# The last 32 of 384 dense tokens of a PEER layer take their up products from gathered rows; one comparison for both one-hots, a gate copy in runs of four, down products in pairs

## The chip, the cores and the metric

The kernel runs on one core of one Trainium2 chip. The metric is the device time of one execution in microseconds (us), the median over several runs. The engines are PE (TensorE: matmuls, with its weight loads as PEld), DVE (VectorE), ACT (ScalarE), POOL (GpSimd) and SP (SyncE, which issues most DMAs). Numbers are fp32. A product of two fp32 operands is computed here as three matmuls of rounded halves: a tensor is split into a rounded part (`_h`, made by ACT) and the rest (`_l`, made by DVE), and h\*h + h\*l + l\*h is summed in PSUM. Only the gate matmuls below take fp32 operands as they are; in the trace four of them leave eight matmul records, two passes each.

## The reference

The program is an encoder of two layers on 512 tokens of 1024 numbers. Layer 1 mixes tokens by neighbourhood attention, layer 2 by a short convolution; each is followed by a PEER channel mixer, which is what the change touches:

```python
q = (xc @ w_query).reshape(c, 8, 2, 128)
sc = jnp.einsum('chpd,hpnd->chpn', q, sub_keys)      # 128 scores on each of two sides
sv, si = lax.top_k(sc, 16)
cand = sv[:, :, 0, :, None] + sv[:, :, 1, None, :]
cidx = si[:, :, 0, :, None] * 128 + si[:, :, 1, None, :]
best, pos = lax.top_k(cand, 16)
eidx = jnp.take_along_axis(cidx, pos, axis=-1)       # 8 x 16 experts of 16384
g = jax.nn.softmax(best, axis=-1)
a = jnp.einsum('cd,chkd->chk', xc, w_up[eidx])
act = jax.nn.gelu(a, approximate=False) * g
return jnp.einsum('chk,chkd->cd', act, w_down[eidx])
```

Each token uses 128 of the 16384 experts; an expert is a row of w_up and a row of w_down.

## The kernel before

A PEER layer (`peer(l)`) treats its 512 tokens, in four chunks of 128, in two ways. The last chunk (`c3`) gathers: for each of its 128 choices k one indirect DMA of POOL fetches a row of w_up per token (`fetch`, `gather_up`), DVE multiplies it with the normed token `hn` and sums, and later a row of w_down is fetched, scaled and added to `accg` (`gather_down`). The 256 gathers of a layer share four buffers `row`. The other 384 tokens (TD) are dense: all 16384 experts are computed for them in 128 blocks of 128 experts, and a gate matrix that is zero for experts that a token didn't choose weighs the results.

A layer runs in these stages, whose times in the first layer are those of the profiled execution:

- Query (309 to 404 us): up matmuls of the query and key scores `ps_k`, and DVE's first top 16.
- Selections (404 to 512): `retrieval()` runs `select` for chunks 3, 0, 1, 2, which is DVE's work throughout (top 16 of the candidates, the two sides `ii` and `jj` of the choice by masks `msk`). For the dense chunks the gates and both sides are transposed into gT, iT and jT.
- Gate stage (512 to 716): 96 quads of four tokens. For each token a one-hot of side i (`ob`) and one of side j scaled by the gate (`oa`) are made, and one matmul of the two gives the token's 128 x 128 gate matrix, in PSUM bank `ps_gb`. ACT copies the four of a quad into `stage`, and every 32 tokens (GT) the stage goes to DRAM as `gd`.
- Experts (732 to 1552): for each block b `dense_up` computes 24 up matmuls (8 slices of 1024 by three products) over 384 columns, and Gelu leaves `ab`. `dense_down` loads the block's gates (`gt`, four blocks in a load), multiplies (`w`), splits w into w_h and w_l, and adds 18 down matmuls of 512 columns into six PSUM accumulators `acc`. `gt` can't be loaded before the last `gd` is written, and the first down matmul waits for that.

Because DVE and ACT are busy in the selections and gates while PE has little to do there, the first NPRE = 52 ups run in those stages, parked in DRAM as `ad` and read back as `at`. Two numbers a step say how much of them PE takes: each step of `retrieval` yields its estimated DVE time and PE time, and ups are emitted until PE's sum reaches PRE_RATE times DVE's. Later ups run AHEAD = 4 blocks ahead of the downs. The lists `fresh` and `kept` interleave blocks computed late and parked blocks. A scheduler then orders each engine's instructions within its limits by pool buffers and dependencies, so that the order on an engine isn't that of the code:

```python
for d, p in retrieval():
    dve += d
    pe += p
    while pe < dve * PRE_RATE and next(pre, 0) is None:
        pe += 0.49
for _ in pre:
    pass
```

Each engine runs its instructions in order, and SP's queue takes all loads of weights, gates and parked blocks in order too; the gathers are issued by POOL.

## Time and profile before

| What | Value |
|---|---|
| median of 3 runs | 3018.89 us (3018.78 to 3021.11) |
| the profiled execution | 3024.75 us |
| its span | 3023.0 us |
| mean granted TensorE clock | 0.996 |
| PE busy | 2978.8 us, 99% |
| DVE busy | 2343.2 us, 78% |
| ACT busy | 1361.7 us, 45% |
| POOL busy | 657.6 us, 22% |
| DMA | 747.94 MB, mean 247 GB/s |

The profile counts an engine as busy from an instruction's start to its end, and matmuls overlap, so the duration of one is longer than the pitch at which they follow each other. Line numbers are those of the kernel printed above. A share over the whole span is a mean over stages that are bound by different things.

### The profile page before, as it was taken

To read this page: it belongs to the slowest core of one execution; us is meant where nothing else is said; L and a number is where in the kernel's file an instruction comes from. 1 tells how busy PE (TensorE), PEld (TensorE's weight loads), DVE (VectorE), ACT (ScalarE), POOL (GpSimd) and SP (SyncE) were. 2 spreads that over 40 slices of the span, in tenths; PEclk is the share of its full clock that TensorE was granted. 3 is DMA by queue.
4 is the path that set the end of the run, shared out by engine and by line. 5 is a ranking of instruction groups with operands and counts; after the bars stand their busy time and mean duration, and the time that the engine had idled before them with its cause. 6 is when DMAs were issued, how large, how long until landed. Compare 5 with 4: busy or idle time off the path is not lost.

```text
span 3023.0 us, 43875 instructions
## 1 busy us (share of the span) xinstructions
PE 2978.8 (99%) x15602; PEld 2665.3 (88%) x15602; DVE 2343.2 (78%) x5115; ACT 1361.7 (45%) x2237; POOL 657.6 (22%) x571
## 2 busy tenths in 40 slices
PE   8999999999999999999999999999999999999998
PEld 6887899999888888888878879999988888888886
DVE  4445899887888888887874489998688888888786
ACT  4444246996333333333342233599733333333333
POOL 0000000001434443443400000000044344444341
PEclk9999999999999999999999999999999999999999
DMA  4332244667999999998943323556699999999994
GB/s 157 98 98 88 95 137 156 228 222 297 337 344 336 336 343 340 338 335 315 331 144 98 108 93 122 163 203 231 246 354 344 333 351 333 338 329 343 331 327 174
DMA packets 297980, 747.94 MB, mean 247 GB/s; under 512 B 23456, under 2 KB 139168, under 8 KB 294688
## 3 DMA queue, kind: packets, MB, share of 16 engines
q1 hardware_dynamic: 224032, 476.67, 45.4%
q0 software_dynamic: 73728, 268.47, 24.0%
q8 instruction: 123, 2.02, 0.3%
q14 instruction: 97, 0.79, 0.1%
HBM read 672.17 MB, written 72.88 MB: 246 GB/s over the span
## 4 chain that ended last, share of the span: by engine, by line
PE 93%; DVE 4%; DMA 1%; issue 1%; ACT 1%; DVEq 0%; ACTq 0%; SPq 0%
PE ps_up L127 46%; PE acc L536 34%; PE ps_gb L457 6%; PE ps_o L191 3%; PE ps_s L261 1%; DVE wu_l L106 1%; PE ps_o L293 1%; PE ps_k L398 1%; PE ps_t L175 1%; PE ps_pt L280 1%; DMA wd_raw<-in_down 1%; DVE tk L595 0%; ACT sq L150 0%; DMA gd<-stage 0%; PE ps_v L239 0%
## 5 line engine op out<-in xcount | busy, mean ns | idle before, releaser
L127 PE MATMUL ps_up<-xhf,wu_l 128*128 128x384 f32 (+1 forms) x2304 | 798.8, 347 | 1.1 <-DVE wu_l L106 1.0
L127 PE MATMUL ps_up<-xhf,wu_h 128*128 128x384 f32 (+1 forms) x2304 | 794.3, 345 | 2.3 <-ACT ab L499 2.0
L127 PE MATMUL ps_up<-xlf,wu_h 128*128 128x384 f32 (+1 forms) x2304 | 792.6, 344 | 0.0
L105 ACT ACTIVATE wu_h<-wu_raw 128x1024 fp32r<-128x1024 f32 x336 | 355.4, 1058 | 712.2 <-PE ps_up L127 435.1
L536 PE MATMUL acc<-wd_h,w_l 128*128 128x512 f32 x1536 | 604.0, 393 | 0.0
L470 POOL DMA_INDIRECT row<-in_up,eidx x256 | 322.3, 1259 | 1277.5 <-DMA wu_raw<-in_up_t 424.7
L536 PE MATMUL acc<-wd_l,w_h 128*128 128x512 f32 x1536 | 599.2, 390 | 0.0
L105 ACT ACTIVATE wd_h<-wd_raw 128x1024 fp32r<-128x1024 f32 x256 | 271.6, 1061 | 703.6 <-issue 619.4
L106 DVE TENSOR_TENSOR wu_l<-wu_raw,wu_h 128x1024 fp32r<-128x1024 f32 x336 | 409.9, 1220 | 172.5 <-ACT wu_h L105 171.2
L536 PE MATMUL acc<-wd_h,w_h 128*128 128x512 f32 x1536 | 516.5, 393 | 2.9 <-ACT w_h L105 2.9
L106 DVE TENSOR_TENSOR wd_l<-wd_raw,wd_h 128x1024 fp32r<-128x1024 f32 x256 | 313.4, 1224 | 241.8 <-ACT wd_h L105 228.8
L127 PEld LDWEIGHTS ps_up<-xhf,wu_h 128*128 128x128 f32 x2304 | 433.3, 188 | 21.8 <-ACT ab L499 3.3
L127 PEld LDWEIGHTS ps_up<-xlf,wu_h 128*128 128x128 f32 x2304 | 433.1, 188 | 17.5
L127 PEld LDWEIGHTS ps_up<-xhf,wu_l 128*128 128x128 f32 x2304 | 433.1, 188 | 17.3 <-DVE wu_l L106 4.0
L470 POOL DMA_INDIRECT row<-in_down,eidx x256 | 329.4, 1287 | 517.7 <-DVE sq L477 470.7
L536 PEld LDWEIGHTS acc<-wd_l,w_h 128*128 128x128 f32 x1536 | 288.5, 188 | 61.9
L536 PEld LDWEIGHTS acc<-wd_h,w_h 128*128 128x128 f32 x1536 | 287.8, 188 | 58.7 <-ACT w_h L105 3.6
L536 PEld LDWEIGHTS acc<-wd_h,w_l 128*128 128x128 f32 x1536 | 288.9, 188 | 54.8 <-DVE w_l L106 0.4
L486 DVE SCALAR_TENSOR_TENSOR accg<-row,ag,accg 128x1024 f32<-128x1024 f32 x256 | 327.4, 1279 | 11.3 <-DMA row<-in_down,eidx 10.5
L477 DVE SCALAR_TENSOR_TENSOR sq<-row,hn 128x1024 bf16<-128x1024 f32 x256 | 311.9, 1218 | 3.7 <-DMA row<-in_up,eidx 2.3
L457 PE MATMUL ps_gb<-ob,oa 128*128 128x128 f32 x1536 | 209.6, 274 | 0.0
L458 ACT ACTIVATE stage<-ps_gb 128x512 f32<-128x512 f32 x192 | 204.6, 1114 | 2.1 <-PE ps_gb L457 1.3
(164 smaller groups left out, 3307.0 us busy)
## 6 DMA issues: line engine op xcount, KB each, us to landing
wd_raw<-in_down SPq DMA_DIRECT2D x256, 512.0 KB
wu_raw<-in_up_t SPq DMA_DIRECT2D x256, 512.0 KB
gd<-stage SPq DMA_DIRECT2D x24, 2048.0 KB
gt<-gd SPq DMA_DIRECT2D x64, 768.0 KB
ad<-ab SPq DMA_DIRECT2D x104, 192.0 KB
at<-ad SPq DMA_DIRECT2D x52, 384.0 KB
...
```

What stands on the lines that cost most here:

```text
L105: nc.scalar.activation(hi, raw, AF.Copy)
L106: nc.vector.tensor_tensor(lo, raw, hi.bitcast(F32), op=ALU.subtract)
L127: nc.tensor.matmul(ps[:, :n], a[:, c], b[:, kc, :n], start=k == 0, stop=k == 3 * KC - 1)
L175: nc.tensor.transpose(ps[k][:, c * P:(c + 1) * P], hs[c][:, kc * P:(kc + 1) * P], ident)
L191: nc.tensor.matmul(ps[c], a[:, m, c * P:(c + 1) * P], b, start=m == 0 and i == 0, stop=m == KC - 1 and i == 2)
L261: nc.tensor.matmul(ps[:, a * 256:(a + 1) * 256], t["q"][hs, j * P:(j + 1) * P], kk[hs, :, BAND0[j]:BAND0[j] + BAND], start=True, stop=True)
L457: nc.tensor.matmul(ps[:, n * NK:(n + 1) * NK], a, b4[:, n], start=True, stop=True)
L458: nc.scalar.activation(stage[:, :, 4 * q:4 * q + 4].rearrange("p i t -> p t i"), ps.rearrange("p (t i) -> p t i", t=4), AF.Copy)
L470: nc.gpsimd.indirect_dma_start(out=t, out_offset=None, in_=table, in_offset=bass.IndirectOffsetOnAxis(ap=eidx[:, k:k + 1], axis=0))
L477: nc.vector.scalar_tensor_tensor(o, t, 1.0, hn, op0=ALU.mult, op1=ALU.mult, accum_out=ag[:, k:k + 1])
L486: nc.vector.scalar_tensor_tensor(accg, t, ag[:, k:k + 1], accg, op0=ALU.mult, op1=ALU.add)
L536: nc.tensor.matmul(acc[c, half], aa[:, cs], ww[:, hs], start=new and i == 0, stop=n == NK - 1 and ww is held[-1][-1])
```

## The change

Of the 384 dense tokens the last 32 (UT) no longer pass through the dense ups, which shrink to TU = 352 columns. Their up products come from gathered rows: partition 32g + t holds token t and the choices of group g, so that 32 indirect DMAs (`urow`) and 32 DVE products with `hu`, the normed tokens in all four quarters, give all 128 choices of 32 tokens. Gelu and gate are applied to these 128 x 32 values, and the result takes the place of the gate in gT; in the down product their `ab` columns are 1.0. So that the ids are there early, the chunk of these tokens (`cu`) is selected first, then c3. The first 36 gathers of c3 (EARLY) follow the 32 in retrieval, in the three buffers that the loads of down rows use later. One DVE comparison of 1024 elements makes both one-hots of a quad, and ACT scales all four. The gate copy writes runs of four tokens and reads PSUM with a stride of 128. 80 ups are parked (NPRE), at a rate of 1.5; gates are loaded for eight blocks at once (GB), and the product w and its split are made for two blocks at once. The reciprocal root of c3's norm is kept and not computed twice. The core of the diff:

```diff
-NPRE = 52
-PRE_RATE = 1.4
+NPRE = 80
+UN = 1
+UT = 32
+TU = TD - UN * UT
+GB = 8
+PRE_RATE = 1.5
 OB = 12
-ACTN = 2
+EARLY = 36
...
+            cu = ND - 1
+            hu = []
+            for u in range(UN):
+                q = slice(P - (UN - u) * UT, P - (UN - u - 1) * UT)
+                t = wpool.tile([P, D], F32, name="hu", tag="wd_h", bufs=2)
+                nc.sync.dma_start(t[q], g_ffn_row[l].to_broadcast([UT, D]))
+                nc.vector.scalar_tensor_tensor(t[q], h[q, cu], rs[cu][q], t[q], op0=ALU.mult, op1=ALU.mult)
+                for g in range(P // UT):
+                    if g * UT != q.start:
+                        nc.scalar.activation(t[g * UT:(g + 1) * UT], t[q], AF.Copy)
+                hu.append((q, t))
...
+            def unit_lists(gg, ii, jj):
+                flat_ids(eid, ii, jj)
+                for u, (q, _) in enumerate(hu):
+                    for g in range(P // UT):
+                        ks = slice(g * UT, (g + 1) * UT)
+                        nc.scalar.activation(fu[ks, u], eid[q, ks], AF.Copy)
+                        nc.scalar.activation(gu[ks, u], gg[q, ks], AF.Copy)
+                nc.vector.tensor_copy(xu, fu)
+            def unit_steps():
+                at = [(u, k) for u in range(UN) for k in range(UT)]
+                for n in range(len(at) + 2):
+                    if n < len(at):
+                        u, k = at[n]
+                        t = wpool.tile([P, D], F32, name="urow", tag="wd_r", bufs=RAW)
+                        nc.gpsimd.indirect_dma_start(
+                            out=t, out_offset=None, in_=up,
+                            in_offset=bass.IndirectOffsetOnAxis(ap=xu[:, u, k:k + 1], axis=0))
+                        urows.append(t)
+                    if n >= 2:
+                        u, k = at[n - 2]
+                        o = acts.tile([P, D], BF16, name="sq", tag="sq")
+                        nc.vector.scalar_tensor_tensor(o, urows.pop(0), 1.0, hu[u][1], op0=ALU.mult, op1=ALU.mult,
+                                                       accum_out=au[:, u, k:k + 1])
+                    yield
+            def unit_values():
+                nc.scalar.activation(au, au, AF.Gelu)
+                nc.vector.tensor_tensor(au, au, gu, op=ALU.mult)
+                ps = ps_acc("ps_u")
+                for u in range(UN):
+                    nc.tensor.transpose(ps[:UT, u * P:(u + 1) * P], au[:, u], ident)
+                for u in range(UN):
+                    for g in range(P // UT):
+                        ks = slice(g * UT, (g + 1) * UT)
+                        nc.scalar.activation(gT[ks, TU + u * UT:TU + (u + 1) * UT],
+                                             ps[:UT, u * P + g * UT:u * P + (g + 1) * UT], AF.Copy)
...
             def retrieval():
-                for c in (3, 0, 1, 2):
+                units = iter(())
+                for c in (cu, c3, 0, 1):
                     it = select(sv[:, c], si[:, c], pr, cand)
                     while True:
                         try:
                             yield next(it), 0.0
+                            for _ in itertools.islice(units, 1):
+                                yield 1.3, 0.0
...
                     else:
                         ps = ps_acc("ps_g")
                         for n, t in enumerate((gg, ii, jj)):
                             nc.tensor.transpose(ps[:, n * P:(n + 1) * P], t, ident)
-                        for n, t in enumerate((gT, iT, jT)):
-                            nc.vector.tensor_copy(t[:, c * P:(c + 1) * P], ps[:, n * P:(n + 1) * P])
+                        for n, t in enumerate((gT, ijT[:, 0], ijT[:, 1])):
+                            m = min(P, TU - c * P) if n == 0 else P
+                            nc.vector.tensor_copy(t[:, c * P:c * P + m], ps[:, n * P:n * P + m])
+                        if c == cu:
+                            unit_lists(gg, ii, jj)
+                            units = itertools.chain(unit_steps(), early_steps())
...
                 for t0 in range(0, TD, GT):
+                    if t0 == TU:
+                        for _ in units:
+                            yield 1.3, 0.0
+                        unit_values()
                     stage = pr.tile([P, NK, GT], F32, name="stage", tag="big")
                     for q in range(GT // 4):
                         ps = ps_acc("ps_gb")
                         t = t0 + 4 * q
-                        b4 = pr.tile([P, 4, NK], F32, name="ob", bufs=OB // 4)
-                        nc.vector.tensor_tensor(b4, iota[:, None, :].to_broadcast([P, 4, NK]),
-                                                iT[:, t:t + 4, None].to_broadcast([P, 4, NK]), op=ALU.is_equal)
-                        a4 = pr.tile([P, 4, NK], F32, name="oa", bufs=OB // 4)
-                        if ACTN:
-                            nc.vector.tensor_tensor(a4[:, :ACTN], iota[:, None, :].to_broadcast([P, ACTN, NK]),
-                                                    jT[:, t:t + ACTN, None].to_broadcast([P, ACTN, NK]),
-                                                    op=ALU.is_equal)
+                        hot = pr.tile([P, 2, 4, NK], F32, name="hot", bufs=OB // 4)
+                        nc.vector.tensor_tensor(hot, iota[:, None, None, :].to_broadcast([P, 2, 4, NK]),
+                                                ijT[:, :, t:t + 4, None].to_broadcast([P, 2, 4, NK]),
+                                                op=ALU.is_equal)
                         for n in range(4):
-                            a, t = a4[:, n], t0 + 4 * q + n
-                            if n < ACTN:
-                                nc.scalar.activation(a, a, AF.Copy, scale=gT[:, t:t + 1])
-                            else:
-                                nc.vector.tensor_scalar(a, iota, jT[:, t:t + 1], gT[:, t:t + 1],
-                                                        op0=ALU.is_equal, op1=ALU.mult)
-                            nc.tensor.matmul(ps[:, n * NK:(n + 1) * NK], a, b4[:, n], start=True, stop=True)
-                        nc.scalar.activation(stage[:, :, 4 * q:4 * q + 4].rearrange("p i t -> p t i"),
-                                             ps.rearrange("p (t i) -> p t i", t=4), AF.Copy)
-                        yield 1.35, 0.9
+                            a = hot[:, 1, n]
+                            nc.scalar.activation(a, a, AF.Copy, scale=gT[:, t + n:t + n + 1])
+                            nc.tensor.matmul(ps[:, n * NK:(n + 1) * NK], a, hot[:, 0, n], start=True, stop=True)
+                        nc.scalar.activation(stage[:, :, 4 * q:4 * q + 4],
+                                             ps.rearrange("p (t i) -> p i t", t=4), AF.Copy)
+                        yield 1.0, 0.9
+                        for _ in itertools.islice(units, 1):
+                            yield 1.3, 0.0
                     nc.sync.dma_start(gd[t0 // GT], stage)
...
+            ring = [pp.tile([P, 2, TD], F32, name=f"ab{n}") for n in range(AHEAD // 2 + 1)]
+            for t in ring:
+                nc.gpsimd.memset(t[:, :, TU:], 1.0)
...
+            def early_steps():
+                uses = []
+                for n in range(EARLY + 2):
+                    if n < EARLY:
+                        fn, k = gathers[n]
+                        uses.append(fn(k, wpool.tile([P, D], F32, name="erow", tag="wd_r", bufs=RAW)))
+                    if n >= 2:
+                        uses.pop(0)()
+                    yield
             def dense_up(b):
-                for ps in up_pieces(up_t[l, b], xh, xl, TD):
+                for ps in up_pieces(up_t[l, b], xh, xl, TU):
                     yield
-                a = pp.tile([P, TD], F32, name="ab", tag="ab", bufs=AHEAD + 2)
-                nc.scalar.activation(a, ps[:, :TD], AF.Gelu)
-                if b < NPRE:
-                    nc.sync.dma_start(ad[b // 2, :, b % 2], a)
-                else:
-                    ab[b] = a
+                a = ring[b // 2 % len(ring)]
+                nc.scalar.activation(a[:, b % 2, :TU], ps[:, :TU], AF.Gelu)
+                if b % 2:
+                    if b < NPRE:
+                        nc.sync.dma_start(ad[b // 2], a[:, :, :TU])
+                    else:
+                        ab[b - 1] = a
...
             def dense_down(n, b):
-                if b % 4 == 0:
-                    gt = p2.tile([P, TD // GT, 4, GT], F32, name="gt")
+                if b % GB == 0:
+                    gt = p2.tile([P, TD // GT, GB, GT], F32, name="gt")
                     nc.sync.dma_start(gt.rearrange("p g i c -> p g (i c)"),
-                                      gd[:, :, b:b + 4].rearrange("g j i c -> j g (i c)"))
+                                      gd[:, :, b:b + GB].rearrange("g j i c -> j g (i c)"))
                     first.append(gt)
-                if b < NPRE and b % 2 == 0:
-                    at = p2.tile([P, 2, TD], F32, name="at")
-                    nc.sync.dma_start(at, ad[b // 2])
-                    ab[b], ab[b + 1] = at[:, 0], at[:, 1]
-                gt = first[-1]
-                w = p2.tile([P, TD], F32, name="w", bufs=1)
-                mark = nc.vector.tensor_tensor(w.rearrange("p (g c) -> p g c", c=GT),
-                                        ab.pop(b).rearrange("p (g c) -> p g c", c=GT), gt[:, :, b % 4], op=ALU.mult)
-                a_h, a_l = split(w, [P, TD], "w", "w", pool=p2)
+                if b % 2 == 0:
+                    if b < NPRE:
+                        at = parked[b // 2 % 2]
+                        nc.sync.dma_start(at[:, :, :TU], ad[b // 2])
+                        ab[b] = at
+                    w = p2.tile([P, 2, TD], F32, name="w", bufs=1)
+                    mark = nc.vector.tensor_tensor(w.rearrange("p i (g c) -> p i g c", c=GT),
+                                            ab.pop(b).rearrange("p i (g c) -> p i g c", c=GT),
+                                            first[-1][:, :, b % GB:b % GB + 2].rearrange("p g i c -> p i g c"),
+                                            op=ALU.mult)
+                    pair.append((mark, *split(w, [P, 2, TD], "w", "w", pool=p2)))
+                mark, a_h, a_l = pair[-1]
+                a_h, a_l = a_h[:, b % 2], a_l[:, b % 2]
...
```

On DVE in the selections of layer 1, before, between two low halves of up blocks (`wu_l`) stand only steps of `select` (msk, pos, tk, best and ds are its tables):

```order
L106 TENSOR_TENSOR wu_l<-wu_raw,wu_h 128x1024
L638 TENSOR_TENSOR msk<-msk,ds 128x2048
L597 MAX_INDEX pos<-best,tk 128x8 x2
L595 MATCH_REPLACE tk<-best,cand 128x60
L643 TENSOR_TENSOR msk<-msk 128x128x8
L624 COPY ds<-sf 128x16
L595 MATCH_REPLACE tk<-best,cand 128x60
L625 TENSOR_TENSOR ds<-sf 128x16x15
L596 MAX best<-tk 128x8
L644 TENSOR_TENSOR msk<-msk 128x128x4
L106 TENSOR_TENSOR wu_l<-wu_raw,wu_h 128x1024
```

After, in the selection that follows, rows gathered in `urow` and multiplied with `hu` stand there too:

```order
L464 SCALAR_TENSOR_TENSOR sq,au<-urow,hu 128x1024
L113 TENSOR_TENSOR wu_l<-wu_raw,wu_h 128x1024
L695 MAX best<-tk 128x8 x3
L737 TENSOR_TENSOR msk<-msk,ds 128x2048
L464 SCALAR_TENSOR_TENSOR sq,au<-urow,hu 128x1024
L696 MAX_INDEX pos<-best,tk 128x8 x3
L113 TENSOR_TENSOR wu_l<-wu_raw,wu_h 128x1024
L742 TENSOR_TENSOR msk<-msk 128x128x8
L723 COPY ds<-sf 128x16
L724 TENSOR_TENSOR ds<-sf 128x16x15
L464 SCALAR_TENSOR_TENSOR sq,au<-urow,hu 128x1024
L694 MATCH_REPLACE tk<-best,cand 128x60 x2
L113 TENSOR_TENSOR wu_l<-wu_raw,wu_h 128x1024
```

From the last key scores to the first gate matmul a layer has 25 wu_l before, and 36 wu_l and 25 products of L464 after; on PE the ups in that stretch go from 601 to 867. On PE at the end of the gate stage of layer 1, before, 95 ups (ps_up) stand between the last gate matmuls (ps_gb) and the first down matmul (acc):

```order
L457 MATMUL ps_gb<-ob,oa 128x128 x4
L127 MATMUL ps_up<-xhf_2453,wu_h 128x384
L127 MATMUL ps_up<-xlf_2454,wu_h 128x384
L127 MATMUL ps_up<-xhf_2453,wu_l 128x384
...
L127 MATMUL ps_up<-xlf_2454,wu_h 128x384
L536 MATMUL acc_7383<-wd_h,w_h 128x512
L536 MATMUL acc_7387<-wd_h,w_h 128x512
```

After, in layer 1, there are 19 ups in that place:

```order
L526 MATMUL ps_gb<-hot 128x128
L134 MATMUL ps_up<-xlf_2454,wu_h 128x352
L526 MATMUL ps_gb<-hot 128x128 x3
L134 MATMUL ps_up<-xhf_2453,wu_l 128x352
...
L134 MATMUL ps_up<-xhf_2453,wu_l 128x352
L631 MATMUL acc_8310<-wd_h,w_h 128x512
L631 MATMUL acc_8314<-wd_h,w_h 128x512
```

And after, in layer 2, none; six down matmuls follow the last two quads, and 14 ups stand behind those:

```order
L526 MATMUL ps_gb<-hot 128x128 x2
L134 MATMUL ps_up<-xlf_15106,wu_h 128x352
L134 MATMUL ps_up<-xhf_15105,wu_l 128x352
L526 MATMUL ps_gb<-hot 128x128 x8
L631 MATMUL acc_20964<-wd_h,w_h 128x512
L631 MATMUL acc_20968<-wd_h,w_h 128x512
...
L134 MATMUL ps_up<-xhf_15105,wu_h 128x352
```

The ups that stood behind the last gates stand ahead of them now, among the gate matmuls: from the first gate to the first down matmul there are 770 ups a layer before and 1222 after.

## Rows read from the trace of the kernel before

**Rows 1.** The page: its span, and the group of the gate matmuls.

```profile
span 3023.0 us, 43875 instructions
...
L457 PE MATMUL ps_gb<-ob,oa 128*128 128x128 f32 x1536 | 209.6, 274 | 0.0
```

**Rows 2.** Windows: length, busy us of PE PEld DVE ACT POOL; clock, DMA, GB/s.

```profile
404.00:512.00 108.00, 106.48 (x608) 104.23 (x607) 107.25 (x478) 62.60 (x77) 0.00 (x0) 1.00 0.50 162
512.00:716.00 204.00, 204.00 (x1448) 203.96 (x1447) 179.74 (x416) 188.58 (x340) 0.00 (x0) 1.00 0.60 216
716.00:732.00 16.00, 16.00 (x94) 16.00 (x93) 4.19 (x5) 5.98 (x8) 4.44 (x4) 1.00 0.89 315
732.00:1490.00 758.00, 758.00 (x3702) 672.99 (x3702) 621.89 (x813) 271.18 (x398) 308.41 (x244) 1.00 0.94 340
...
1725.00:1800.00 75.00, 69.56 (x334) 58.15 (x333) 56.36 (x245) 25.72 (x43) 1.46 (x2) 0.95 0.32 102
```

**Rows 3.** Timeline of PE: start, us, engine, line; below, a group.

```profile
1001.72 0.39 PE L536 MATMUL acc<-wd_h,w_h 128*128 128x512 f32 x1
...
1005.84 0.33 PE L127 MATMUL ps_up<-xhf,wu_h 128*128 128x384 f32 x1
...
1010.02 0.39 PE L536 MATMUL acc<-wd_h,w_h 128*128 128x512 f32 x1
...
2161.54 1.06 PE L457 MATMUL ps_gb<-ob,oa 128*128 128x128 f32 x8
...
L127 PE MATMUL ps_up<-xhf,wu_h 128*128 128x384 f32 x2048 | 693.2, 338 | 2.0 <-ACT ab L499 2.0
```

**Rows 4.** Timeline of DVE.

```profile
598.82 1.22 DVE L106 TENSOR_TENSOR wu_l<-wu_raw,wu_h 128x1024 fp32r<-128x1024 f32 x1
599.96 0.68 DVE L443 TENSOR_TENSOR ob<-iota,iT 128x512 f32<-128x512 f32 x1
600.56 0.42 DVE L447 TENSOR_TENSOR oa<-iota,jT 128x256 f32<-128x256 f32 x1
600.90 0.60 DVE L455 TENSOR_SCALAR oa<-iota,jT,gT 128x128 f32<-128x128 f32 x2
```

**Rows 5.** Timeline of ACT; below, a group.

```profile
604.25 1.06 ACT L105 ACTIVATE wu_h<-wu_raw 128x1024 fp32r<-128x1024 f32 x1
605.22 0.68 ACT L453 ACTIVATE oa<-oa,gT 128x128 f32<-128x128 f32 x2
605.80 0.47 ACT L499 ACTIVATE ab<-ps_up 128x384 f32<-128x384 f32 x1
606.17 2.05 ACT L458 ACTIVATE stage<-ps_gb 128x512 f32<-128x512 f32 x2
...
L395 ACT ACTIVATE qpT<-ps_up 128x512 f32<-128x512 f32 x32 | 18.6, 580 | 0.0
```

**Rows 6.** Timeline of all engines, from the last gates to the first downs.

```profile
716.08 1.13 ACT L458 ACTIVATE stage<-ps_gb 128x512 f32<-128x512 f32 x1
...
730.91 0.53 ACT L105 ACTIVATE w_h<-w 128x384 fp32r<-128x384 f32 x1 [1.59 <-issue]
...
2169.15 1.13 ACT L458 ACTIVATE stage<-ps_gb 128x512 f32<-128x512 f32 x1
...
2184.76 0.56 DVE L520 TENSOR_TENSOR w<-ab,gt 128x384 f32<-128x384 f32 x1 [5.67 <-DMA gt<-gd]
...
2185.98 1.66 PE L536 MATMUL acc<-wd_h,w_h 128*128 128x512 f32 x6 [0.40 <-ACT w_h L105]
```

**Rows 7.** DMA from 800 to 1400 us, in 40 slices of 15 us.

```profile
GB/s 284 348 373 320 332 371 323 334 382 283 338 364 353 317 377 338 298 365 284 365 342 365 320 381 309 312 361 313 355 307 323 365 326 340 343 363 315 353 240 359
DMA packets 85302, 201.61 MB, mean 336 GB/s; under 512 B 6030, under 2 KB 39822, under 8 KB 85261
```

**Rows 8.** Groups of DVE's products with gathered rows.

```profile
L486 DVE SCALAR_TENSOR_TENSOR accg<-row,ag,accg 128x1024 f32<-128x1024 f32 x256 | 327.4, 1279 | 11.3 <-DMA row<-in_down,eidx 10.5
L477 DVE SCALAR_TENSOR_TENSOR sq<-row,hn 128x1024 bf16<-128x1024 f32 x256 | 311.9, 1218 | 3.7 <-DMA row<-in_up,eidx 2.3 <-DVE w_l L106 0.3
```

70 lines of the change are left out of this document (42 added, 28 removed).

## The prediction

> **What bounds the kernel now.** I read the page's busy shares first, in the table above: the reader is to see that TensorE (PE) is busy nearly the whole span and VectorE (DVE) most of it. An average hides the stages, so I cut the first layer's retrieval and experts into windows [rows 2]. In the selections (404 to 512 us) PE is busy 106.5 of 108 us, but DVE 107.25: both are full. In the gate stage (512 to 716) PE is full, DVE has 24 us and ScalarE (ACT) 15 us left. In the experts (732 to 1490) PE is full and the DMA engines are at 0.94. Wherever PE is full, its own pitch is the price of an instruction, so I took pitches from the timeline rather than mean durations, which overlap [rows 3]. Last I looked at what the changed lines cost on DVE and ACT [rows 4, 5] and at the step from the last gates to the first down matmul [rows 6].
>
> The profiled execution took 3024.75 us (span 3023.0 [rows 1] and 1.75 around it), 5.86 above the median of the runs, 3018.89. I sum against 3024.75 and take 5.86 off at the end.
>
> **1. Columns: -84 us.** An up matmul goes from 384 to 352 columns. Pitch now: 18 down matmuls of 512 columns fill 1001.72 to 1005.84, 228.9 ns each; 24 ups of 384 fill 1005.84 to 1010.02, 174.2 ns each [rows 3]. The slope is 54.7/128 = 0.427 ns a column, so 32 columns are 13.7 ns and the new pitch 160.5. There are 3 x 2048 = 6144 such matmuls [rows 3]: 84 us. The other bound uses the gate passes: 8 passes of 128 columns in 1.06 us, of which the last takes the group's mean of 0.274 [rows 1, 3], so a pitch of 0.112; the slope from there to 384 is 0.243, and the gain 48 us. I take 84, since 352 lies beside 384 and 512. Wherever PE is not the last to finish, this gain isn't had.
>
> **2. Selections: +12 us.** Ahead of the first gate matmul, the order has 601 ups before and 867 after; DVE gets 36 low-half splits for 25, and 25 products with gathered rows. A split occupies 1.14 us of DVE (598.82 to 599.96), and lasts 1.22; a product with a gathered row lasts 1.22 too [rows 4, 8]. DVE's other work there is 107.25 - 25 x 1.14 = 78.8. After: 78.8 + 61 x 1.14 = 148.3 us, against 867 x 0.1605 = 139.2 for PE. PE waits 9.1 us for low halves; now it waits about 108 - 601 x 0.1742 = 3.3. Two layers: 2 x 5.8 = +12. If the products hide in idle DVE time that I don't see, 0; if the list copies and the id sums each stall DVE, +16.
>
> **3. Gate stage: 0.** After, a layer has 384 gate matmuls (768 passes x 0.112 = 86 us) and some 1200 ups (193 us): PE 279 us. DVE: 96 quads, each with one comparison of 1024 elements. No row has it; those of 512 and 256 occupy 0.60 and 0.34 [rows 4], hence 0.26 per 256 and 1.12 to 1.2 for 1024, which I take as 1.14. 109 us, 50 splits 57, some 45 products 51, the rest of the last selection 15: 232, covered by PE with 47 to spare. ACT: 384 scales x 0.30 and the splits and Gelus of 50 blocks x (0.97 + 0.37) make 182 [rows 5], and the gate copy decides the rest. The copy occupies 0.92 to 1.1 now (two in 2.05); 512 contiguous elements from PSUM take 0.58, about 0.49 with overlap [rows 5]. The new copy writes runs of four elements and reads PSUM with a stride of 128. No row here shows such a read by ACT, so its bounds are 0.49 and 0.94. With 0.49 ACT needs 229, with 0.94 272: covered on the whole either way, hence 0. I take the fast end, because contiguous source with scattered destination is what costs 1.1 now, and the destination is what improves; the slow end is a rival.
>
> [...]
>
> **4. The step from gates to experts: +38 us, cover gone.** The first down needs the chain last gate copy, store of gd, load of gt, product w, rounding w_h. In layer 2 this runs from the copy's start at 2169.15 by w at 2184.76, where gt's load ended 5.67 us of waiting, to the down at 2185.98: 16.8 us. In layer 1 it is 716.08 to the end of w_h at 731.44: 15.4 [rows 6]. Now 95 ups lie behind the last gate (16 us of PE work, the row 716 to 732 [rows 2]) and PE waits 0.40 in layer 2 and not at all in layer 1. After, the order has 19 ups there in layer 1 and none in layer 2. The chain also changes: gt carries 1536 KB, 768 more, +2.5 us (+2.0 at 382 GB/s, the highest slice [rows 7]; +6 if one queue is slow), the rounding takes 768 elements, +0.7, the copy gains 0.4: +2.8. PE's idle time is 15.4 + 2.8 - 19 x 0.1605 = 15.1 in layer 1 and 16.8 + 2.8 = 19.6 in layer 2: 34.3 more than now's 0.4. [...] I put 2 us a layer. Together +38. The bounds are +30 (no clock loss, a short gt) and +47.
>
> **5. DMA in the experts without ups: +2 us.** 80 blocks are parked instead of 52, so the last three groups of eight in each layer run on downs alone, 8 x 18 x 0.2289 = 33 us of PE for a group. A group needs eight times 0.524 MB of down rows, about 10.5 gathered tiles of 0.524, a gt of 1.57 and parked tiles of 1.44: 12.7 MB, or 385 GB/s. The stretch 800 to 1400 moved 336 GB/s on average with slices up to 382 [rows 7]. The groups before have ups, in which loads run ahead, so I take +2; held to 356 it is 2.7 a group, +16; if all fits, 0. The paired w and its split lie under the down matmuls of the block before, the norm that is saved and ACT's three copies for hu under the query's matmuls, and the transposes of the new values take 0.2 us of PE: 0.
>
> **Sum.** -84 + 12 + 0 + 38 + 2 = -32: 2992.7 profiled, and less 5.86 a median of 2987.
>
> **The rivals.**
> - *The gate copy stays slow* (0.94 us). The average hides the end: of the last 40 quads in layer 1 the order has 347 ups, PE 347 x 0.1605 + 320 x 0.112 = 92 us, but ACT 156 x 0.30 + 40 x 0.94 + 15 x 0.97 + 14 x 0.37 = 104; the last 48 of layer 2 give 106 against 122. Together +28: 3015. For it: nothing shows the strided read. Against: the present cost lies with scattered writes.
> - *The covers hold* better than I count: DVE keeps pace in the selections, and PE finds its ups ahead of the chain's end (a shorter gd and gt trip). Then the other terms come to 5 to 30 in place of 52: 2940 to 2965. The chain of 15 us was measured beside traffic of the row at 0.89 DMA share [rows 2], so an idle start could be quicker.
> - *Gathers late: slower than before.* DVE takes its instructions in order, so a product that waits for its row holds the splits behind it, and PE waits for those. A layer has 68 such gathers, 25 of them in the selections, where DVE has nothing to spare. 50 waits of x us cost 50x; it decides against the change (+0.2% over now) where x is over (32 + 6)/50 = 0.8 us. At 1 us: 3037. Against it: in the experts 244 gathers in 758 us share four buffers, a turn of 4 x 758/244 = 12.4 us [rows 2], and all their DVE waits are 2.3 + 10.5 us [rows 8]; after, three buffers turn in 3 x 148.3/25 = 17.8 us. For it: three buffers are fewer than four, and DVE has no slack there to take a late row.
> - *DMA is the limit* in the last groups: at 336 GB/s a group takes 37.8 us for 33.0, six of them +29 in place of 2: 3014. The mean of [rows 7] speaks for it, its slices above 370 against.
> - *A column is cheap.* At the slope of 0.243 from the gate passes [rows 1, 3] the first term is -48 and the time 3023. The pitches at 384 and 512 columns speak against it [rows 3]. [...]
>
> **How the numbers follow.** Forecast 0.50 (2965 to 3000 by the bounds of terms 2, 4 and 5), slow gate copy 0.18, covers hold 0.15, late gathers 0.11, DMA limit 0.04, cheap columns 0.02. 0.2% is 6 us and about what a measurement of this kernel can tell from no change: faster is below 3012.9, slower above 3024.9. The forecast, the covers, two fifths of the slow copy and a little of the rest are faster, 0.75; a third of the slow copy, half of the DMA limit and a little of the forecast are the same, 0.11; the rest, 0.14, is slower. Leaving out one in ten at either side goes from 2948 (inside the covers case) to 3018 (just past the slow copy).
>
> **What would show it.** Right: ups at a pitch of 160 ns; PE idle 15 and 19 us ahead of the first down, ended by w_h; PE waiting for wu_l in the selections for about 9 us a layer; a gate copy near 0.6 us; DVE's comparison at 1.2 us. Wrong: a gate copy at 1.1 with ACT ending PE's waits late in the gate stage; DVE waiting on the gathered rows; PE waiting on wd tiles late in the experts, ended by DMA; or a step of under 8 us.

## The result, and the profile after

The changed kernel takes 3050.97 us in the median (3046.76 to 3052.97, four runs), before 3019.18 in runs on the same chip: a ratio of 1.0102, with a 95% interval of 1.0085 to 1.012. It is slower by 1%, where 2987 was forecast. Its profiled execution took 3052.97 us. The page's first lines, and its DMA total:

```profile
span 3051.2 us, 43374 instructions
...
PE 2911.4 (95%) x15604; PEld 2591.3 (85%) x15604; DVE 2332.0 (76%) x4410; ACT 1380.0 (45%) x2519; POOL 818.8 (27%) x645
...
DMA packets 278680, 798.50 MB, mean 262 GB/s; under 512 B 24064, under 2 KB 118272, under 8 KB 275392
```

PE is busy 67 us less, and the span is 28 us longer: the gain was had and more than lost in waits. 50.6 MB more are moved. The windows of layer 1 by stages (selections, gate stage, step, two halves of the experts, and 20 us behind the last down matmul; columns as in [rows 2]):

```profile
407.10:559.90 152.80, 145.76 (x877) 142.35 (x876) 147.37 (x531) 80.00 (x108) 34.14 (x28) 0.98 0.76 256
559.90:840.20 280.30, 279.87 (x1976) 279.26 (x1975) 229.28 (x242) 235.61 (x585) 59.52 (x40) 1.00 0.81 294
840.20:863.10 22.90, 3.34 (x23) 3.05 (x21) 2.24 (x4) 2.56 (x4) 3.99 (x6) 0.64 0.92 340
863.10:1207.90 344.80, 344.80 (x1678) 299.76 (x1679) 280.04 (x318) 121.69 (x153) 153.06 (x106) 0.99 0.93 337
1207.90:1552.70 344.80, 340.57 (x1587) 289.14 (x1586) 282.81 (x322) 119.73 (x146) 147.16 (x105) 0.99 0.95 340
1552.70:1572.70 20.00, 0.42 (x2) 0.00 (x0) 15.55 (x18) 2.32 (x4) 6.69 (x9) 0.59 0.64 212
```

The last row is the one to look at: behind the last down matmul PE does nothing, while DMA still moves 212 GB/s and DVE works on gathered rows. Before, layer 1 ended differently: DMA was at 0.94 in the experts, too [rows 2], but at 0.65 in the last 62 us, beside a full PE:

```profile
1490.00:1552.00 62.00, 62.00 (x278) 51.37 (x277) 46.36 (x64) 24.48 (x35) 10.52 (x8) 1.00 0.65 226
```

PE's waits over the whole span after the change say the same (us in total, times, longest), as does its timeline at that place:

```profile
PE acc L631 <- ACT w_h L112: 38.0, 2, 19.6
PE ps_t L183 <- DVE r L160: 37.8, 3, 24.3
PE acc L631 <- ACT wd_h L112: 8.5, 2, 4.3
PE ps_up L134 <- DVE wu_l L113: 8.5, 11, 1.5
PE ps_up L134 <- ACT ab L588: 8.4, 8, 2.2
```

```profile
1552.72 0.40 PE L631 MATMUL acc<-wd_l,w_h 128*128 128x512 f32 x1
1577.38 3.03 PE L183 MATMUL ps_t<-ident,hs 128*128 128x128 f32 x12 [24.26 <-DVE r L160]
```

The first wait is the step from gates to experts. The second is the start of layer 2, whose norm needs chunk 3, and that waits for the last gathered row; POOL issued it 12 us after the last down matmul:

```profile
1565.08 1.86 POOL L544 DMA_INDIRECT row<-in_down,eidx  x1 [2.34 <-DVE accg L563]
```

Three pieces came out as forecast: the pitch of an up matmul (24 fill 905.34 to 909.18, 160.0 ns), the gate copy (589 ns for 1114; its group in the kernel before stands last) and the comparison (1222 ns):

```profile
905.34 0.32 PE L134 MATMUL ps_up<-xhf,wu_h 128*128 128x352 f32 x1
...
909.18 0.39 PE L631 MATMUL acc<-wd_h,w_h 128*128 128x512 f32 x1
...
L520 DVE TENSOR_TENSOR hot<-iota,ijT 128x1024 f32<-128x1024 f32 x192 | 231.2, 1222 | 63.8 <-PE ps_gb L526 63.6
L527 ACT ACTIVATE stage<-ps_gb 128x512 f32<-128x512 f32 x192 | 109.1, 589 | 8.9 <-PE ps_gb L526 7.2 <-DMA gd<-stage 1.0
```

```profile
L458 ACT ACTIVATE stage<-ps_gb 128x512 f32<-128x512 f32 x192 | 204.6, 1114 | 2.1 <-PE ps_gb L457 1.3
```

Since the change moves ups between stages, I take from each stage's length (between first and last matmuls in the trace) PE's work in it at these pitches (for the gate matmuls of a layer the prediction's 86 us), and compare what is left, which I call a stage's loss, both layers together:

| Where | Forecast | Measured |
|---|---|---|
| columns, 6144 x 14.2 ns | -84 | -87 |
| selections (152.8 and 156.6 us for 139 of work) | +12 | +24 |
| gate stage | 0 | +3 |
| step from gates to experts (19.9 and 18.7 us idle) | +38 | +38 |
| waits among the down matmuls | +2 | +11 |
| layer 2's start, waiting for the last gathers | 0 | +24 |
| the end of the span, the same | 0 | +12 |
| start of layer 1, query | 0 | +3 |
| sum | -32 | +28 |

### The profile page after: what moved, and what is told of

It is laid out like the page before. It is cut to its first block, busy times and chain, and to the rows that moved or that the text cites. A ratio compares the mean times of both kernels' runs of the same rounds, so it can differ in the third digit from the quotient of the medians.

```text
span 3051.2 us, 43374 instructions
## 1 busy us (share of the span) xinstructions
PE 2911.4 (95%) x15604; PEld 2591.3 (85%) x15604; DVE 2332.0 (76%) x4410; ACT 1380.0 (45%) x2519; POOL 818.8 (27%) x645
## 5 line engine op out<-in xcount | busy, mean ns | idle before, releaser
L134 PE MATMUL ps_up<-xhf,wu_h 128*128 128x352 f32 (+1 forms) x2304 | 774.0, 336 | 12.0 <-ACT ab L588 8.4
L134 PE MATMUL ps_up<-xhf,wu_l 128*128 128x352 f32 (+1 forms) x2304 | 774.8, 337 | 8.8 <-DVE wu_l L113 8.5
L134 PE MATMUL ps_up<-xlf,wu_h 128*128 128x352 f32 (+1 forms) x2304 | 770.5, 334 | 0.0
L631 PE MATMUL acc<-wd_h,w_h 128*128 128x512 f32 x1536 | 604.8, 396 | 46.5 <-ACT w_h L112 38.0
L631 PE MATMUL acc<-wd_l,w_h 128*128 128x512 f32 x1536 | 497.1, 392 | 0.0
L134 PEld LDWEIGHTS ps_up<-xlf,wu_h 128*128 128x128 f32 x2304 | 437.1, 190 | 14.2
L544 POOL DMA_INDIRECT row<-in_down,eidx x224 | 311.9, 1393 | 415.9 <-DVE sq L553 373.2
L563 DVE SCALAR_TENSOR_TENSOR accg<-row,ag,accg 128x1024 f32<-128x1024 f32 x224 | 286.9, 1281 | 11.5 <-DMA row<-in_down,eidx 10.7
L520 DVE TENSOR_TENSOR hot<-iota,ijT 128x1024 f32<-128x1024 f32 x192 | 231.2, 1222 | 63.8 <-PE ps_gb L526 63.6
L553 DVE SCALAR_TENSOR_TENSOR sq<-row,hn 128x1024 bf16<-128x1024 f32 x216 | 263.6, 1220 | 6.7 <-DMA row<-in_up,eidx 5.8
L525 ACT ACTIVATE hot<-hot,gT 128x128 f32<-128x128 f32 x768 | 242.2, 393 | 34.8 <-DVE hot L520 32.6
```

The lines of the kernel that those rows point to most:

```text
L134: nc.tensor.matmul(ps[:, :n], a[:, c], b[:, kc, :n], start=k == 0, stop=k == 3 * KC - 1)
L520: nc.vector.tensor_tensor(hot, iota[:, None, None, :].to_broadcast([P, 2, 4, NK]), ijT[:, :, t:t + 4, None].to_broadcast([P, 2, 4, NK]), o ...
L525: nc.scalar.activation(a, a, AF.Copy, scale=gT[:, t + n:t + n + 1])
L544: nc.gpsimd.indirect_dma_start(out=t, out_offset=None, in_=table, in_offset=bass.IndirectOffsetOnAxis(ap=eidx[:, k:k + 1], axis=0))
L553: nc.vector.scalar_tensor_tensor(o, t, 1.0, hn, op0=ALU.mult, op1=ALU.mult, accum_out=ag[:, k:k + 1])
L563: return lambda: nc.vector.scalar_tensor_tensor(accg, t, ag[:, k:k + 1], accg, op0=ALU.mult, op1=ALU.add)
```

## The experiments

Theory A is that the DMA engines' supply is the limit of the changed experts stage, and that the gathers, served last, end late. Theory B is that the gathers are late for another reason: the turn of their four buffers, or their place in the order. All medians stand beside 3019 to 3022 us of the kernel before on the same chip.

**Fewer bytes, no other work less.**

```diff
-                if b % GB == 0:
+                if b % GB == 0 and n // GB % 2 == 0:
                     gt = p2.tile([P, TD // GT, GB, GT], F32, name="gt")
```

> The changed kernel, with every second load of a group's gates left out (the group is weighed with the gates of the group before it, so that part of the result is not the reference's): about 12.6 MB less in each layer's experts, and no gather, no product and no matmul less. Theory A (the DMA engines' supply is the limit of the changed experts stage, and the gathers, which are last to be served, end late): at the 338 GB/s of that stage 12.6 MB are 37 us, more than the 21 us that layer 2's start and the 12 us that the end now wait for the last gathers, so both waits go and so do some 10 us of waits among the down matmuls: about 3010. Theory B (the gathers end late because four buffers turn too slowly, or because of their place in the order): nothing changes, 3045 to 3055.

Measured: 3006.76 us (ratio 0.9956, 0.9942 to 0.997). The windows at the end of layer 1's experts and behind them:

```profile
1500.00:1543.00 43.00, 43.00 (x191) 35.23 (x189) 30.86 (x36) 17.14 (x22) 4.76 (x5) 1.00 0.55 190
1543.00:1560.00 17.00, 14.40 (x64) 11.61 (x63) 11.03 (x30) 7.98 (x17) 0.19 (x4) 0.80 0.06 17
```

DMA is done before PE, PE goes on at once, and both end waits are gone. 44 us come back for bytes that no gather needs, as theory A has it.

**More buffers for the gathers.**

```diff
-RING = 4
+RING = 8
```

> The changed kernel with eight buffers for the gathered rows in the experts instead of four. Theory A (DMA supply): the same bytes at the same rate, 3045 to 3055. Theory B (turn of the buffers): the gathers run ahead, the waits for the last of them at the end of both layers (21 and 12 us) go: about 3018.

Measured: 3059.85 us (1.0132, 1.0116 to 1.0149). Its last windows:

```profile
1400.00:1500.00 100.00, 91.82 (x387) 74.48 (x386) 81.55 (x94) 30.17 (x36) 46.52 (x35) 0.95 0.95 350
1500.00:1573.00 73.00, 72.67 (x317) 58.86 (x315) 51.38 (x58) 27.88 (x33) 5.34 (x3) 1.00 0.57 188
```

The gathers now end early (188 GB/s in the last window), but PE stops 8 us in the window ahead, its waits for halves of down rows (`wd_h`) come to 25.3 us in place of 8.5, and the last down matmul comes at 1572.7 instead of 1552.7. What the gathers win the down rows lose, so theory B, which asked for 3018, falls. The turn of four buffers does hold the rate back a little: from 900 to 1500 us it is 336 to 362 GB/s in stretches of 100 us here and 335 to 349 in the changed kernel.

**The cover held.** The ups of the first five unparked blocks are tied behind the last gate matmul:

```diff
-                            nc.tensor.matmul(ps[:, n * NK:(n + 1) * NK], a, hot[:, 0, n], start=True, stop=True)
+                            gate.append(nc.tensor.matmul(ps[:, n * NK:(n + 1) * NK], a, hot[:, 0, n], start=True, stop=True).ins)
...
-                    for _ in ups(nup, top):
-                        pass
+                    with tc.issue_after(gate[-1]) if n == 0 else nullcontext():
+                        for _ in ups(nup, top):
+                            pass
```

> The changed kernel, with the ups of the first five blocks that are not parked tied behind the last gate matmul: 122 ups (19.5 us of TensorE) lie between gates and downs where the changed kernel has 19 and none. If the idle time ahead of the first down (20 and 19 us) is the lost cover, it goes almost wholly and the gate stage is as much shorter: -35, about 3016, whether the experts are bound by DMA or not, since they start earlier. If the gate stage is bound by something other than TensorE, or if a shorter gate stage only lets the DMA fall further behind, less than half of it is seen: over 3034.

Measured: 3046.5 us (1.0093, 1.0073 to 1.0113). The end of layer 1's gate stage, the step, and the end of the experts:

```profile
800.00:831.00 31.00, 24.55 (x151) 22.43 (x150) 21.58 (x19) 30.94 (x96) 0.00 (x0) 0.94 0.41 165
831.00:851.00 20.00, 20.00 (x127) 19.88 (x127) 5.96 (x6) 7.76 (x12) 4.00 (x6) 1.00 0.83 310
...
1550.00:1578.00 28.00, 4.15 (x22) 3.43 (x21) 21.43 (x43) 6.65 (x15) 7.05 (x11) 0.57 0.45 154
```

PE is busy through the step, but the experts begin 12 us sooner and not 20. Without those ups among them the last quads run at ACT's pace, 30.94 of 31 us, and PE waits for scaled one-hots (7.1 us in the stage): the gate stage takes 268 us for 251 of PE's work (1031 ups and the gate matmuls), a loss of 17 us where the changed kernel has 2. In the experts stand 70 more ups, 11 us, so the last down matmul moves by only 3 us, and the wait behind it stays. So the gate stage gives the step's gain back, which is the expectation's case of a stage that another engine than PE sets; the loss among the down matmuls is no larger than in the changed kernel (8 us for 9), so that DMA takes the gain back there is not shown.

**Products out of the selections: an edit that left them there.** The steps of the gathered rows are no longer called between steps of `select`.

```diff
                             yield next(it), 0.0
-                            for _ in itertools.islice(units, 1):
-                                yield 1.3, 0.0
```

> The changed kernel, with the products of the gathered rows taken only in the gate stage, none in the selections. If VectorE is the limit of the selections, their 153 and 157 us fall to what TensorE needs for 867 ups, 139 us, so about -30; the order also has 103 ups behind the last gate, so the idle time ahead of the first down falls from 20 and 19 us to 2 to 4, another -35 by the theory of the lost cover. VectorE's 232 us in the gate stage become some 260, still under TensorE. The waits at the end of the layers stay or grow if DMA supply is their cause, since fewer bytes have moved before: 2985 to 3000. If VectorE becomes the limit of the gate stage, the gain of the selections is given back there: 3015 or more.

Measured: 3055.98 us (1.0117, 1.0098 to 1.0137), with selections of 152.1 and 155.6 us: the scheduler had moved the products forward again (25 in layer 1's selections, as in the changed kernel), so this run tells nothing of the selections. It did put 102 ups behind the last gates, and PE's idle time in the step fell from 20 to 7 us; but the gate stage's loss rose by 11 and 8 us, and the waits behind the last down matmuls from 24 and 23 to 29 and 31. The run that ties each product behind a quad's comparison does tell of the selections:

```diff
-                        nc.vector.tensor_tensor(hot, iota[:, None, None, :].to_broadcast([P, 2, 4, NK]),
+                        mark = nc.vector.tensor_tensor(hot, iota[:, None, None, :].to_broadcast([P, 2, 4, NK]),
...
-                        for _ in itertools.islice(units, 1):
-                            yield 1.3, 0.0
+                        with tc.issue_after(mark.ins):
+                            n = len(list(itertools.islice(units, 1)))
+                        yield 1.3 * n, 0.0
```

> The run that was to take the products of gathered rows in the gate stage alone left the selections at 152 and 156 us, since the scheduler moved them back; here each is tied behind the comparison of a quad, so none is left in the selections (651 and 675 ups there instead of 867, 69 and 70 behind the last gates). If the products and splits on VectorE set the length of the selections, that falls to 110 to 118 us, and the gate stage grows by some 25. TensorE's stages sum to 20 us a layer less. If DMA supply binds from the gate stage on, part is given back, since the gathers start later: 3010 to 3045. If the selections stay over 140 us, something else than VectorE's products set them.

Measured: 3041.9 us (1.0075, 1.0058 to 1.0092). Selections and gate stage of layer 1, and the 20 us behind its last down matmul:

```profile
408.10:516.30 108.20, 106.89 (x661) 105.15 (x659) 107.53 (x476) 66.43 (x85) 4.60 (x3) 1.00 0.58 186
516.30:835.80 319.50, 311.89 (x2139) 309.82 (x2140) 267.19 (x296) 246.78 (x606) 101.47 (x65) 0.99 0.86 314
1544.20:1564.20 20.00, 0.39 (x2) 0.00 (x0) 15.03 (x20) 1.69 (x3) 10.97 (x9) 0.58 0.75 247
```

So DVE's products were what made PE wait in the selections: these are back at 108 us, with 650 ups for 866 and PE idle 1.4 us for 7.0. The gate stage takes the products at a loss of 14 and 10 us, for 2 and 1, which eats most of what the selections gain; some 70 ups behind the last gates halve PE's idle time in the step. The wait at the end is longer than in the changed kernel (29.4 us for 24.3, DMA at 247 GB/s for 212): the last down matmul comes 8.5 us sooner, but the last gather is issued only 3.5 us sooner.

**Gathers moved out of the experts**, without and with the cover held.

```diff
-EARLY = 36
+EARLY = 56
```

> The changed kernel with 56 instead of 36 of a layer's 256 gathers of the last chunk taken in retrieval: 20 x 0.524 = 10.5 MB a layer leave the experts, whose DMA is full at 338 GB/s, and enter the gate stage, which moves 294 GB/s at a share of 0.81. Theory A (DMA supply limits the changed experts): 31 us of transfer less a layer, so the waits for the last gathers (21 and 12 us) and most of the 10 us among the down matmuls go: 3005 to 3020. If the experts are limited by something else, or the 20 products (24 us of VectorE) hold up the gate stage, where TensorE has 50 us more work than VectorE: over 3040.

> As the run with 56 early gathers, and the ups of the first five unparked blocks tied behind the last gate matmul as in the run that held the cover. That run gave only 4 us: by theory A because the experts were then bound by DMA and took back what the earlier start gave. With 10.5 MB less a layer there, the cover should now be worth what TensorE's idle time says, 15 to 20 us a layer: 2970 to 2990. If the cover is worth nothing by itself, this stays at the time of the run with 56 early gathers.

Measured: 3047.05 us (1.0088, 1.0071 to 1.0105) and 3054.66 (1.0108, 1.0091 to 1.0125). Gate stage and end of the first of them:

```profile
558.90:853.50 294.60, 287.74 (x1995) 285.92 (x1993) 253.82 (x278) 236.60 (x589) 101.21 (x60) 0.99 0.88 319
1559.90:1579.90 20.00, 15.85 (x73) 12.59 (x72) 11.99 (x32) 9.10 (x18) 0.20 (x4) 0.83 0.05 15
```

The end waits are gone as theory A has it, and the gate stage is 14 and 18 us longer. With the cover held as well, PE is idle 18 us of that stage, so what the step gains is lost there again. The size was a miss: the gate stage had no 20 products and 10 MB to spare.

**Fewer parked blocks, cover held.**

```diff
-NPRE = 80
+NPRE = 72
...
-PRE_RATE = 1.5
+PRE_RATE = 1.4
```

> The changed kernel with the cover held and 72 instead of 80 parked blocks: eight blocks of ups (31 us of TensorE) go from the gate stage back to the experts, with the same weights' bytes there (4.2 MB) and 2.8 MB less for parking. Theory A: TensorE's work in the experts is then 727 us for some 247 MB, 340 GB/s, just at the supply, instead of 685 us for 243 MB; the gate stage falls to some 220 us, which VectorE just allows. Waits at the ends shrink: 2975 to 3000. If VectorE or ACT, not TensorE, sets the gate stage, or if DMA fills up there too: 3010 to 3035.

Measured: 3046.64 us (1.0082, 1.0065 to 1.0099). The last gates of layer 1:

```profile
760.00:813.00 53.00, 41.03 (x255) 37.00 (x255) 35.80 (x30) 52.94 (x164) 0.00 (x0) 1.00 0.38 160
```

The end waits are gone here too, but the gate stage takes 251 us for some 220 of PE's work: without ups among them, the last quads run at ACT's pace, 52.94 of 53 us; it scales all four one-hots of a quad now, and two before.

**The change in two parts.** First the columns without the rows (352 columns, no gathered rows and no products for the 32 tokens), then the rest without either (`UN = 0`, 384 columns); in both, early gathers begin after the last chunk's selection:

```diff
...
                         nc.vector.tensor_copy(g3, gg)
+                        units = early_steps()
...
-                            unit_lists(gg, ii, jj)
-                            units = itertools.chain(unit_steps(), early_steps())
...
```

> The changed kernel without the gathered rows of the 32 tokens and their products: their columns stay out of the ups, but nothing takes their place (the gates stand where the activations belong, so the last 32 dense tokens of the result are not the reference's). All else of the change stays. Theory A (the gathers' bytes cost what the columns give): 33.5 MB and 64 products less, TensorE's 84 us are had in full: 2930 to 2960. If the rest of the change (80 parked blocks, eight blocks of gates in a load, the order of the selections) is what costs: 3000 or more.

> The rest of the change alone: all 384 dense tokens pass through the dense ups again, no rows are gathered for 32 of them; the comparison for both sides, the gate copy in runs of four, 80 parked blocks, gates for eight blocks in a load, products in pairs, 36 early gathers and the selections' new order stay (early gathers begin after the last chunk's selection). Theory A: TensorE's work is that of the kernel before, and the experts' DMA has 16.8 MB a layer less to move than in the changed kernel, so TensorE is the limit again: 3015 to 3035. If the rest of the change is what costs: 3050 to 3100.

Measured: 3006.05 us (0.9955, 0.9938 to 0.9971) and 3070.42 (1.0163, 1.0146 to 1.018). Neither is as theory A alone has it. The difference of the two is the columns: 64 of 87 us. From the first to the changed kernel are the rows and their products: 3050.97 - 3006.05 = +45, of which 31 are waits behind the last down matmuls (3.9 and 13.1 us in that run, 24.3 and 23.4 in the changed kernel). And the rest by itself costs 51. Its selections, gate stage and step in layer 1:

```profile
408.50:537.20 128.70, 121.01 (x686) 117.53 (x686) 122.22 (x494) 68.63 (x87) 22.27 (x16) 1.00 0.65 214
537.20:815.00 277.80, 271.63 (x1824) 270.70 (x1824) 200.59 (x197) 227.31 (x566) 37.66 (x20) 0.99 0.70 250
815.00:870.20 55.20, 48.70 (x268) 47.87 (x268) 18.28 (x18) 16.68 (x24) 6.87 (x6) 0.94 0.77 279
```

Each loses 8 to 11 us (264 ups of 174.2 ns are 46 of the step's 55); in layer 2 it is 10 in the selections, 1 in the gate stage and 10 in the step. The experts themselves lose little here, 5 and 6 us, for 2 and 6 in the kernel before.

**What of the rest costs.** On top of the last:

```diff
-NPRE = 80
+NPRE = 56
...
-PRE_RATE = 1.5
+PRE_RATE = 1.4
...
-EARLY = 36
+EARLY = 0
```

> Of the change only what moves no bytes and no products: the comparison for both sides, the fast gate copy, products in pairs, gates for eight blocks in a load, the selections' new order; no rows are gathered for the 32 tokens (384 columns), no early gathers, 56 parked blocks at the rate 1.4. Theory: what costs in the rest of the change (+51 us alone) is early gathers in the selections and the ups that go ahead of the gates with them, so that the cover is lost or late; without both, TensorE's work is that of before and it is covered: 3010 to 3030. If the loads of eight blocks or the selections' order cost: 3045 or more.

Measured: 3026.08 us (1.0019, 1.0009 to 1.0029), 44 less. The merged comparison, the fast copy, the pairs, the larger gate loads, the selections' order and four more parked blocks together cost 6 us and bring nothing; early gathers and the 24 further parked blocks cost the rest. Which of these two was not tried apart.

**A version that balances.** Tied products with `EARLY = 56`; the same with ACT's rounding of the first w tied behind the fifth unparked block's Gelu; and `EARLY = 48` with that tie and the cover held:

```diff
-                nc.scalar.activation(a[:, b % 2, :TU], ps[:, :TU], AF.Gelu)
+                gelu[b] = nc.scalar.activation(a[:, b % 2, :TU], ps[:, :TU], AF.Gelu).ins
...
-                    pair.append((mark, *split(w, [P, 2, TD], "w", "w", pool=p2)))
+                    with tc.issue_after(gelu[NPRE + AHEAD]) if n == 0 else nullcontext():
+                        pair.append((mark, *split(w, [P, 2, TD], "w", "w", pool=p2)))
```

> The products of the 32 tokens tied into the gate stage (as in the tied run) and 56 early gathers, so that the gate stage's DMA is in use to its end and the experts have 10.5 MB less. By the stages of those two runs: selections 108 to 111 us, gates 325, experts 670 to 690 without a wait for the last gathers: 1125 to 1140 a layer for the changed kernel's 1168, so 2985 to 3015, at or under the kernel before. By DMA: 366 MB a layer, 20 of them in the selections, the rest at 338 GB/s make 1131 us, the same. If gathers and splits together stall VectorE in the gate stage (88 products in 96 quads), that stage exceeds 340 us and the time stays over 3030.

> The tied kernel with 56 early gathers, with one more tie: ACT's rounding of the first w stands behind the Gelu of the last cover block, instead of ahead of Gelus that TensorE waits for. In the run without the tie, TensorE had 172 and 167 ups (27 us) behind the last gates and yet was idle for 25 us there, while ACT stood at w_h waiting for the gates' load and the Gelu that frees the ups' PSUM bank stood behind it. If that order is the cause: -25 us a layer, the step from gates to experts takes what its ups take, 28 to 32 us, and the time is 2980 to 3000, under the kernel before. If the loads of weights behind the gates' load are what is late, the wait moves there: over 3025.

> The tied kernel with 48 early gathers, the first five unparked blocks held behind the last gates and the rounding of the first w behind their Gelus. By stages: selections 108 to 111, gate stage some 290 (TensorE 285, VectorE 281), the step 28 us of ups, experts 688 us with 237 MB, 345 GB/s, so some 10 us of waits for the last gathers by theory A: 2975 to 3005. With 48 instead of 56 early gathers the gate stage is shorter and the experts are nearer to the DMA's supply than in the run with 56: if it is slower than that run by over 5 us, the experts' DMA is still what counts.

Measured: 3041.39 us (1.0082, 1.0062 to 1.0103), 3045.84 (1.0088, 1.0065 to 1.0111) and 3027.19 (1.0027, 1.0015 to 1.0039). The tie of w changed nothing: PE's wait for Gelus behind the last gates is still there in the second,

```profile
PE ps_up L134 <- ACT ab L587: 52.6, 3, 27.1
```

so the reason given for it falls. The order has 172 ups there, over seven blocks, while the three pair buffers of `ab` hold six; that the later ones wait for a buffer that only w frees is argued, not shown. In the third the end waits are gone and the step takes 40 us for 27 of ups. Last, without the tie of w, the cover cut to five blocks (the next block's ups tied behind the first down matmul), with 48 and 56 early gathers, and then, with 48, buffers of their own for the gathered rows, three (and two for the one-hots) or two:

```diff
-                    with tc.issue_after(gate[-1]) if n == 0 else nullcontext():
+                    with tc.issue_after(gate[-1] if n == 0 else accs[0]) if n < 2 else nullcontext():
...
-                        t = wpool.tile([P, D], F32, name="urow", tag="wd_r", bufs=RAW)
+                        t = p2.tile([P, D], F32, name="urow", tag="grow", bufs=RAW)
```

> The tied kernel with 48 early gathers and a cover of just five blocks: the first five unparked blocks' ups (120) behind the last gates, and the next block's ups tied behind the first down matmul. In the run before it, 168 ups stood there, and TensorE waited 9.5 us a layer for weights of the last of them, whose loads stand in SP's queue behind the load of the gates; the step took 40 us. If a cover that SP has loaded before the gates' load is what is wanted: the step falls to 20 to 25 us, PE idles 2 to 5 us in it, 10 to 13 us less a layer: 3000 to 3012, under the kernel before. If the gate stage, whose last quads ACT sets, takes it back: 3020 or more.

> The same with 56 early gathers: 4.2 MB a layer less in the experts and eight products more (10 us of VectorE) in the gate stage. If the experts' DMA still costs: some us faster than with 48. If VectorE or the gathers' waits set the gate stage: 5 to 15 us slower than with 48.

> The run with 48 early gathers and a cover of five blocks, in which the gathered rows of retrieval have three buffers of their own instead of those of the down rows' loads (and the one-hots two buffers instead of three, to make room). In that run TensorE stood 15 us a layer ahead of the first down matmul behind the weights' half wd_h, whose row can be loaded only when the last early gather's product has given its buffer back; with 56 early gathers it stood 38. If that sharing is what is left of the step: it falls from 35 to 20 to 23 us, and the down rows are there when the gates' load lands: 3036 - 26 = 3005 to 3015, under the kernel before. If the gates' load itself takes that long beside the gathers, the wait goes over to w_h and the time stays over 3025.

> The same with two buffers for the gathered rows and three for the one-hots, as before. If the one-hots' third buffer is worth more than a third row: faster than the run with three by up to 10 us. If a gather needs the turn of three buffers (some 3 us a quad, landing times included): the products wait for their rows, the gate stage grows by over 10 us, and it is slower.

Measured: 3036.48 us (1.0055, 1.0039 to 1.0071), 3089.19 (1.0201, 1.018 to 1.0222), 3043.21 (1.007, 1.0056 to 1.0083) and 3142.55 (1.0394, 1.038 to 1.0409). PE's wait ahead of the first down ("issue" is one that ends with nothing that the profile names), of the first, second and third (there with its largest wait, and ended by w_h):

```profile
PE acc L632 <- issue: 30.3, 2, 15.2
```

```profile
PE acc L632 <- issue: 75.9, 2, 38.1
```

```profile
PE ps_gb L525 <- ACT hot L524: 34.5, 30, 3.0
...
PE acc L632 <- ACT w_h L112: 7.4, 2, 3.8
```

Eight more gathers make that wait 23 us a layer longer, and three buffers of their own bring it down to 4, as the expectation has it: the first down rows can't be loaded while early gathers hold the three buffers that both share. The time went back into the gate stage, where PE waits 34.5 us for scaled one-hots, and 17.8 in the first of the four. That run changes the rows' buffers and the one-hots' together, so it doesn't tell which of them costs this. With two row buffers and three for the one-hots it is worse still, and the wait ahead of the first down is back, now for w_h:

```profile
PE acc L632 <- ACT w_h L112: 61.3, 2, 32.0
```

From the start of layer 1's gate stage to 860 us DVE waits 56 us for gathered rows there, and 18 with three buffers, so two are too few for the gathers. No version with the whole change was faster than the kernel before; the nearest is the third of the group above, at 1.0027.

## Why the prediction was wrong

- **Term 1** was right: -87 for -84. That PE would have the gain "wherever it is the last to finish" was the condition that failed.
- **Term 2** was mis-sized: +24 for +12. The mechanism (DVE full with splits and products) is shown by the tied run; what the sum lacked are DVE's waits for gathered rows, 4.4 us in layer 1 and 6.8 in layer 2, and PE's for Gelus on ACT, 5.0 and 3.5. That the latter follow from the former is argued.
- **Term 3** was right, gate copy and comparison included, and with it the rival of the slow copy falls. That the copy gains nothing was so too, since PE sets that stage (busy 279.87 of 280.3 us).
- **Term 4** was nearly right in size. The table's +38 is idle time alone, where 34 and 4 of clock were forecast. But the run with the cover held shows that ups moved there don't bring the 38 back: the gate stage, which then lacks them, takes most of it. No run shows the clock's 2 us a layer as such, an estimate of the author's ([rows 2] has 75 us with 5.4 us idle at a mean clock of 0.95); the changed kernel shows 1.9 a layer, which stand in the table's row of the down matmuls: behind 19.6 us without work the first ten matmuls ran at a granted clock of 0.50 and took 3.9 us for 2.0 at the pitches above, in layer 2, behind 18.4 us, again at 0.50 and 3.9:

```profile
863.09:866.98 3.89, 3.89 (x10) 3.31 (x11) 2.94 (x4) 1.49 (x3) 0.00 (x0) 0.50 0.88 321
```

- **Term 5 is the step that failed**, and with it the sum: +2 was forecast, and +43 measured (24 and 12 behind the last down matmuls and, without the clock's 4, 7 among them). It asked for the rate of the last three groups of eight only, and put the price on PE's waits for down rows. The whole stage was to be summed: 128 down rows' tiles (67 MB), 41 fresh blocks (983 ups in the stage, 21 MB), 220 gathers (115), gates (25) and parked blocks (14) are 243 MB; at the 338 GB/s of the windows that is 719 us, and PE's work there is 685. The stage with its tail, to the last product with a gathered row, lasts 709. That these bytes are what costs is shown by the run without 12.6 MB of gates a layer (-44 us, no end waits) and by the 20 gathers moved out (no end waits either). [rows 2] had the row for it: DMA at 0.94 and 340 GB/s beside a full PE, in a stage whose PE time the change cut by 17% while its bytes fell by 13% (272 MB from the first to the last down matmul before, 238 with the tail after). And the shortage shows only in small part where I looked: the weights come nearly in time, the gathers lag, and the wait falls at the start of the next layer and at the end of the span.
- **The rivals.** "DMA is the limit" was the right one, at 0.04, and it was priced at 3014 from six groups. "Gathers late" named the wrong gathers and the wrong place: of its 50 waits in the selections DVE had seven, 11 us in all, and those that cost most were down rows at the end of a layer.
- **The range** took its bounds from PE's side. Its upper end, 3000, is that of terms 2 and 4; with term 5's own bound of +16 it would have been 3014. A second resource at 0.94 wants a bound of its own: 719 - 685 = 34 us a layer.

The mean of 338 is not that of every stretch: those of 100 us in the experts lie between 317 and 362, slices of 15 us reach 382 [rows 7], and the 49 us behind the step in the run with the cover held 379. At 355 GB/s the 243 MB would take PE's 685 us (an estimate from those two numbers), and the late gathers would not follow, so the measured 338 decides. It is what this mix of transfers had in this order.

What stays open: which of early gathers and parked blocks costs more in the rest of the change, why ups behind the last gates waited for Gelus in the tied runs, and what sets 338 where other stretches reach 379.
